# Weight sums made by adding transfers, with their products half a chunk pair later, in the output projection of a hybrid decoder layer

## Chip, cores and metric

The kernel runs on one core of one Trainium2 chip. The metric is device microseconds (us) of one execution of the whole program, lower is better.

## What is computed

One decoder layer over 256 positions of width 4096: a normalized input is projected to 13,328 columns, four head groups (retention, block attention, a state-space branch, a linear recurrence) mix them, and the four gated results, together 4096 wide, go through one output projection. The residual is added and a last RMSNorm follows. The change lies in the output projection alone, the last two lines here:

```python
h = rms_norm(x, norm_w)
proj = jnp.einsum('bsd,de->bse', h, w_in)
...
y = jnp.concatenate([y_ret, y_moba, y_ssm, y_lru], axis=-1)
return x + jnp.einsum('bse,ed->bsd', y, w_out)
```

## The kernel before

Everything is float32. To use the fast matmul type fp32r, each operand is split in two fp32r halves: a high part (a copy that rounds, made by ACT) and a low part (operand less high part, made by DVE). A product takes three matmuls: high by high, low by high, high by low. `split` (L159) does this for the weights, in `high_low` (L172): ACT casts at L173, DVE subtracts at L174. The activations `yhl` are split before.

Weights stream from memory in chunks of 128 partitions by 1024 float32 columns (512 KB); a chunk is two blocks, each of 128 rows of the weight matrix by 512 of its columns. `load` (L137) issues a chunk's transfer on SP's queue into one of five buffers `raw` (`RAW`, L24), `split` turns it into a pair `whi`, `wlo`, of which there are three (`SPL` + 1). The main loop at chunk n issues first the split of chunk n+2 and the load of chunk n+5, then the matmuls of chunk n.

The output projection does two blocks of 512 output columns at once (`pair`, L834; o = 0, 2, 4, 6, from `FAST`, L31). For each of 16 steps c over the contraction there are two chunks, i = 0 and 1, one for each column block. A plain step multiplies both chunks by both halves of the positions: 12 matmuls of 512 columns for each chunk, 24 a step. A *fast* step (c in `FAST[o]`, 18 in all) sees the 2 by 2 blocks of activations and of weights as a matrix product of Strassen and Winograd's form: seven block products in place of eight, so 21 matmuls. It needs four sums of weight blocks, which DVE makes in place in the two raw buffers (L186, L187, L189, L191), and their own splits `thi`, `tlo` (L188, L190, L192, L193: the casts and subtractions are again those of L173 and L174). The sums of activations are made once, in `mix_y` (L769), into tiles `ys`. Every three matmuls are one call of `three` (L786 to L792).

After the 16 steps `early` (L845) has mixed the products into the residual, by two operations a chunk from the queue `side`, and `row` (L802) finishes each block. POOL's queue brings the residual x and the last norm's weights (`extra`, L822) into tiles `xres` and `fw`. The last pair (o = 6) keeps the splits of its last chunks ("hold") and does half of their products at the end, beside the norm of the other half.

A scheduler sets the order of the instructions on each engine, from the order in which the program is written and its own idea of durations; on the chip each engine takes its instructions strictly in that order, and waits where one is not ready.

Of the kernel before, what the change touches and what calls it, by code (L numbers as in the profile page):

```python
# [32 lines left out]
LATE = 13  # L33
EPS = 1e-6
# [61 lines left out]
def tile_kernel(ctx: ExitStack, tc: tile.TileContext, t: dict):  # L96
# [19 lines left out]


    chunks = []
    for gi, (what, cols) in enumerate(GROUPS):
        w = len(cols)  # L120
        for c in range(NCH):
            src = t[f"w{gi}"][c]
            if gi == 0:
                chunks += [("x", src[:, k * w:(k + 1) * w], KC * c + k, 1, w) for k in range(KC)]
            else:
                chunks.append(("in", src, KC * c, KC, w))
    for o in FAST:
        for c in range(NCH):
            for i in range(2):
                where = "fast" + "ab"[i] if c in FAST[o] else "hold" if o == NO - 2 and LATE <= c + i / 2 < LATE + 1.5 else "out"  # L130
                chunks.append((where, t["wo"][o + i, c], KC * c, KC, 512))
    raws, xraws, parts = {}, {}, {}

    def b4():
        return br.tile([P, 4, S], F32, name="b4", bufs=4)
# [23 lines left out]
    def split(n):  # L159
        if n >= len(chunks):  # L160
            return
        where, _, kt, nk, w = chunks[n]
        if where == "x":
            split_x(xraws.pop(n))
        raw = raws.pop(n)
        if where == "hold":
            hi, lo = pair_of(mixed[0], "t", 4, 1024)
        else:
            hi, lo = pair_of(wp, "w", SPL + 1, WW)
        parts[n] = hi, lo  # L170

        def high_low(h, l, raw, a, b):  # L172
            A.copy(h[:, a:b], raw[:, a:b])  # L173
            V.tensor_tensor(l[:, a:b], raw[:, a:b], h[:, a:b].bitcast(F32), ALU.subtract)  # L174

        cuts = FIRST if n == 0 else CUTS if n == 1 else ((512, 1024),) if where == "fastb" else ((0, nk * w),)
        for a, b in cuts:
            high_low(hi, lo, raw, a, b)
        if where == "fasta":
            raws["a"] = raw  # L180
        elif where == "fastb":

            ra, rb = raws.pop("a"), raw
            (ha, la), (hb, lb) = (pair_of(mixed[0], "t", 4, 1024) for _ in range(2))
            c1, c2 = slice(0, 512), slice(512, 1024)
            V.tensor_tensor(ra[:, c1], rb[:, c1], ra[:, c1], ALU.subtract)  # L186
            V.tensor_tensor(rb[:, c1], rb[:, c2], rb[:, c1], ALU.subtract)  # L187
            high_low(ha, la, ra, 0, 512)  # L188
            V.tensor_tensor(rb[:, c2], rb[:, c2], ra[:, c1], ALU.subtract)  # L189
            high_low(hb, lb, rb, 0, 512)  # L190
            V.tensor_tensor(ra[:, c2], ra[:, c2], rb[:, c2], ALU.subtract)  # L191
            high_low(hb, lb, rb, 512, 1024)  # L192
            high_low(ha, la, ra, 512, 1024)  # L193
            parts[n, "t"] = (ha, la), (hb, lb)

    def pair_of(pool, tag, bufs, size):
        return [pool.tile([P, size], F32R, name=tag + x, bufs=bufs) for x in ("hi", "lo")]
# [571 lines left out]
    def mix_y(c):  # L769
        ya, yb = yhl[KC * c], yhl[KC * c + 1]  # L770
        q = mixed[0].tile([P, 512], F32, name="ma")
        for i, y in enumerate((ya, yb)):
            V.tensor_tensor(q[:, i * 256:(i + 1) * 256], y[:, 0:256].bitcast(F32), y[:, 256:512].bitcast(F32), ALU.add)
        a11, a21, a12, a22 = (q[:, i * P:(i + 1) * P] for i in range(4))
        s = mixed[0].tile([P, 512], F32, name="mb")
        s1, s2, s3, s4 = (s[:, i * P:(i + 1) * P] for i in range(4))
        V.tensor_tensor(s1, a21, a22, ALU.add)
        V.tensor_tensor(s2, s1, a11, ALU.subtract)
        V.tensor_tensor(s3, a11, a21, ALU.subtract)
        V.tensor_tensor(s4, a12, s2, ALU.subtract)  # L780
# [13 lines left out]
    def tile_y(kt, e):  # L794
        return yhl[kt][:, e * P:(e + 1) * P], yhl[kt][:, 256 + e * P:256 + (e + 1) * P]
# [6 lines left out]
    def row(o, k, ps, xres, fw, at, a=0, b=512):  # L802

        V.tensor_tensor(xres[:, a:b], xres[:, a:b], ps[:, a:b], ALU.add)
        A.activation(ps[:, a:b], xres[:, a:b], AF.Square, accum_out=fss[:, k, at:at + 1])
        V.tensor_tensor(rs[k][:, o * 512 + a:o * 512 + b], xres[:, a:b], fw[:, a:b], ALU.mult)

    def store(k):

# [24 lines left out]
    def pair(o, n, q, r, spare):  # L834
# [5 lines left out]
        held = {}  # L840

        def add(out, a, b):
            side.append(lambda: V.tensor_tensor(out, a, b, ALU.add))  # L843

        def early():  # L845

            u = mixed[0].tile([P, 512], F32, name="ma")
            w = mixed[0].tile([P, 512], F32, name="mb")
            side.append(lambda: A.copy(u, p1))
            add(x11, x11, u)  # L850
            add(u, u, p6)
            add(w, u, p7)
            add(x12, x12, u)
            add(x12, x12, p5)
            add(x21, x21, w)
            add(x22, x22, w)
            add(x22, x22, p5)
            if end:
                add(x22, x22, q[3])

        for c in range(NCH):
            if o == 0 and 1 <= c <= len(MIX):
                mix_y(MIX[c - 1])
            for i in range(2):
                split(n + SPL)
                load(n + RAW)
                for _ in range(2):
                    if side:
                        side.popleft()()
                p = parts.pop(n)  # L870
                tt = parts.pop((n, "t"), None)
                n += 1
                if c in fast:
                    first, last = c == fast[0], c == fast[-1]
                    hl = ysum[c]
                    mix = lambda j: (hl[:, j * P:(j + 1) * P], hl[:, 512 + j * P:512 + (j + 1) * P])
                    if i == 0:
                        three(p1, tile_y(KC * c, 0), p, 0, first, last)
                        three(q[0], tile_y(KC * c + 1, 0), p, 512, False, False)
                    else:  # L880
                        three(q[1], mix(3), p, 512, False, False)
                        three(p5, mix(0), tt[0], 0, first, last)
                        three(p7, mix(2), tt[1], 0, first, last)
                        three(p6, mix(1), tt[1], 512, first, last)
                        three(q[2], tile_y(KC * c + 1, 1), tt[0], 512, False, False)
                else:
                    mms(q[i], 0, c, p, c == 0, c == NCH - 1)
                    if end and c >= LATE:
                        held[c, i] = p
# [15 lines left out]
        row(o + 1, 0, q[1], x12, fw2, NO, 256, 512)  # L905
        done()
        for c in range(LATE, NCH):
            mms(q[2], 1, c, held[c, 0], False, c == NCH - 1)
        row(o, 1, q[2], x21, fw1, o)
        for j, a in enumerate((0, 256)):  # L910
            for c in range(LATE, NCH):
                mms(spare[j], 1, c, held[c, 1], c == LATE, c == NCH - 1, a, a + 256)
# [6 lines left out]
    MIX = (7, 9, 12, 2, 4)  # L919
# [53 lines left out]
```

## Time and profile before

| what | before |
| --- | --- |
| median of 3 runs | 1558.94 us (1558.78 to 1559.57) |
| profiled execution, its own time | 1558.47 us |
| its span, first to last instruction | 1556.7 us |
| PE (matmul) busy | 1541.6 us, 99% of the span |
| DVE busy | 954.6 us, 61% |
| ACT busy | 779.3 us, 50% |
| DMA, mean over the span | 200 GB/s |

The span is read stage by stage: the output projection fills its last 340 us or so. Busy shares say which engine is full; the order of an engine's instructions, and what each waits for, say whether another engine can keep it full.

### The profile page before, as it was taken

The numbers are of one execution on the slowest core, as the hardware profiler recorded it, in microseconds if no ns is written. First come the engines' busy times: TensorE is split into PE (matmuls) and PEld (weight loads), VectorE is DVE, ScalarE is ACT, GpSimd is POOL, SyncE is SP. The second block draws the span as 40 slices with busy tenths as digits, with TensorE's granted clock in tenths as the row PEclk, the third lists the DMA queues.
The fourth block names the chain that finished last, engine by engine and source line by source line (L and its number), as shares of the span: only waits on it lengthen the run. The fifth ranks groups of instructions, "written<-read, shape, count | busy, mean of one in ns | idle before, by whom it ended". The sixth has DMA issues, their size and how long they took to land.

```text
span 1556.7 us, 19182 instructions
## 1 busy us (share of the span) xinstructions
PE 1541.6 (99%) x7202; PEld 1286.7 (83%) x7202; DVE 954.6 (61%) x1233; ACT 779.3 (50%) x1019; POOL 28.7 (2%) x56
## 2 busy tenths in 40 slices
PE   9999999999999999999999999999999999999996
PEld 8988888888888788888888888888888888888885
DVE  5564444485565644545556757444447888887878
ACT  5644444454455434444448845444446555554553
POOL 0000000000000100000000000000000000000000
PEclk9999999999999999999999999999999999999999
DMA  8965555555555655545555455555555656576764
GB/s 310 333 223 179 183 178 184 178 190 189 199 187 187 207 184 189 176 170 176 185 197 182 170 196 176 196 188 189 189 195 190 220 206 238 190 234 213 235 219 168
DMA packets 89134, 311.20 MB, mean 200 GB/s; under 512 B 10304, under 2 KB 11984, under 8 KB 89040
## 3 DMA queue, kind: packets, MB, share of 16 engines
q1 hardware_dynamic: 83808, 296.70, 54.7%
q0 software_dynamic: 3360, 10.51, 2.3%
q10 hardware_dynamic: 1872, 2.76, 0.5%
q8 instruction: 56, 0.92, 0.2%
q14 instruction: 38, 0.31, 0.1%
HBM read 305.71 MB, written 4.22 MB: 199 GB/s over the span
## 4 chain that ended last, share of the span: by engine, by line
PE 97%; DVE 1%; issue 1%; DMA 0%; ACT 0%; POOL 0%; ACTq 0%; POOLq 0%; DVEq 0%
PE pm L712 24%; PE pm L710 24%; PE pm L711 24%; PE pm L792 4%; PE pm L790 4%; PE pm L791 4%; PE pb L791 3%; PE pb L792 3%; PE pb L790 3%; PE pb L287 1%; PE pb L711 0%; PE pb L712 0%; PE pb L710 0%; DMA b<-in_xt 0%; DVE xres L843 0%
## 5 line engine op out<-in xcount | busy, mean ns | idle before, releaser
L174 DVE TENSOR_TENSOR wlo<-raw,whi 128x1024 fp32r<-128x1024 f32 (+3 forms) x545 | 650.7, 1198 | 540.3 <-ACT whi L173 518.1
L173 ACT CAST whi<-raw 128x1024 fp32r<-128x1024 f32 (+3 forms) x545 | 558.6, 1029 | 642.1 <-PE pm L711 494.8
L710 PE MATMUL pm<-whi,xT 128*128 128x512 f32 (+1 forms) x1664 | 645.7, 388 | 1.1 <-ACT whi L173 1.1
L712 PE MATMUL pm<-wlo,xT 128*128 128x512 f32 (+1 forms) x1664 | 642.4, 386 | 0.9 <-DVE wlo L174 0.9
L711 PE MATMUL pm<-whi,xT 128*128 128x512 f32 (+1 forms) x1664 | 641.7, 386 | 0.0
L712 PEld LDWEIGHTS pm<-wlo,xT 128*128 128x128 f32 x1664 | 312.5, 188 | 64.5 <-DVE wlo L174 1.7
L710 PEld LDWEIGHTS pm<-whi,xT 128*128 128x128 f32 x1664 | 312.9, 188 | 63.6 <-ACT whi L173 1.6
L711 PEld LDWEIGHTS pm<-whi,xT 128*128 128x128 f32 x1664 | 312.8, 188 | 62.0
L791 PE MATMUL pm<-whi,xT 128*128 128x512 f32 (+1 forms) x218 | 84.1, 386 | 0.0
L790 PE MATMUL pm<-whi,xT 128*128 128x512 f32 (+1 forms) x218 | 84.0, 385 | 0.0
L792 PE MATMUL pm<-wlo,xT 128*128 128x512 f32 (+1 forms) x218 | 84.0, 385 | 0.0
L791 PE MATMUL pb<-whi,xT 128*128 128x512 f32 x178 | 69.2, 389 | 0.0
L792 PE MATMUL pb<-wlo,xT 128*128 128x512 f32 x178 | 69.2, 389 | 0.0
L790 PE MATMUL pb<-whi,xT 128*128 128x512 f32 x178 | 69.2, 389 | 0.0
L173 ACT CAST thi<-raw 128x512 fp32r<-128x512 f32 (+1 forms) x75 | 45.8, 636 | 33.1 <-DVE raw L186 19.9
L174 DVE TENSOR_TENSOR tlo<-raw,thi 128x512 fp32r<-128x512 f32 (+1 forms) x75 | 52.0, 708 | 0.2
L790 PEld LDWEIGHTS pm<-whi,xT 128*128 128x128 f32 x218 | 41.0, 188 | 8.2
L791 PEld LDWEIGHTS pm<-whi,xT 128*128 128x128 f32 x218 | 41.0, 188 | 8.2
L792 PEld LDWEIGHTS pm<-wlo,xT 128*128 128x128 f32 x218 | 41.0, 188 | 8.1
L791 PEld LDWEIGHTS pb<-whi,xT 128*128 128x128 f32 x178 | 33.4, 188 | 7.0
L792 PEld LDWEIGHTS pb<-wlo,xT 128*128 128x128 f32 x178 | 33.4, 188 | 7.0
L790 PEld LDWEIGHTS pb<-whi,xT 128*128 128x128 f32 x178 | 33.4, 188 | 7.0
(252 smaller groups left out, 957.4 us busy)
## 6 DMA issues: line engine op xcount, KB each, us to landing
raw<-in_w SPq DMA_DIRECT2D x384, 512.0 KB, 3.5
raw<-in_wo SPq DMA_DIRECT2D x128, 512.0 KB, 5.0
raw<-in_w SPq DMA_DIRECT2D x31, 520.0 KB, 4.5
b<-in_x SPq DMA_DIRECT2D x8, 512.0 KB, 5.5
xres<-in_x POOLq DMA_DIRECT2D x16, 256.0 KB, 5.4
b<-in_xt SPq DMA_DIRECT2D x15, 257.0 KB, 4.5
fw<-in_fnw POOLq DMA_DIRECT2D x8, 256.0 KB, 5.5
out<-rs ACTq DMA_DIRECT2D x8, 256.0 KB, 2.9
```

The lines of the kernel that those rows point to most:

```text
L173: A.copy(h[:, a:b], raw[:, a:b])
L174: V.tensor_tensor(l[:, a:b], raw[:, a:b], h[:, a:b].bitcast(F32), ALU.subtract)
L287: T.transpose(ps[:, e * S + k * P:e * S + (k + 1) * P], tk[k][:, (2 * u + e) * P:(2 * u + e + 1) * P], ident)
L710: T.matmul(ps[:, :w], xh, hi[:, o:o + w], start=first, stop=False)
L711: T.matmul(ps[:, :w], xl, hi[:, o:o + w], start=False, stop=False)
L712: T.matmul(ps[:, :w], xh, lo[:, o:o + w], start=False, stop=last)
L790: T.matmul(ps, x[0], hi, start=first, stop=False)
L791: T.matmul(ps, x[1], hi, start=False, stop=False)
L792: T.matmul(ps, x[0], lo, start=False, stop=last)
```

## The change

The change does five things. (1) The lists `FAST` become 6, 8, 10, 12 for the first pair and 2, 4, 6, 8, 10, 12 for the others: 22 fast steps. (2) Two of the four weight sums of a fast step are no longer made by DVE: right behind the split of the first chunk, `split` issues two transfers on POOL's queue with `accum_op=ALU.add`, which read one block of 512 columns (256 KB) of the second chunk again from memory and add it to the first 512 columns of each raw buffer. The signs of the activation sums and of `early` are adapted. (3) The other two sums and the four splits move to `sums_of`, called at the second chunk; the four products that use them run after the plain matmuls of the following chunk, step c+1, i = 0. (4) `RAW` is 7 in place of 5, since a fast step's raw buffers are held longer; there are three pairs of `t` tiles in place of four. (5) For room, `xres` is no tile of its own but a slice of the result `rs`, and three of the held chunks of the last pair use `t` and old `ys` tiles.

```diff
-SPL, RAW, WARM = 2, 5, 28
+SPL, RAW, WARM = 2, 7, 28
...
-FAST = {0: (7, 9, 12), 2: (2, 4, 7, 9, 12), 4: (2, 4, 7, 9, 12), 6: (2, 4, 7, 9, 12)}
+FAST = {0: (6, 8, 10, 12), 2: (2, 4, 6, 8, 10, 12), 4: (2, 4, 6, 8, 10, 12), 6: (2, 4, 6, 8, 10, 12)}
...
         if where == "fasta":
-            raws["a"] = raw
-        elif where == "fastb":
-
-            ra, rb = raws.pop("a"), raw
-            (ha, la), (hb, lb) = (pair_of(mixed[0], "t", 4, 1024) for _ in range(2))
-            c1, c2 = slice(0, 512), slice(512, 1024)
-            V.tensor_tensor(ra[:, c1], rb[:, c1], ra[:, c1], ALU.subtract)
-            V.tensor_tensor(rb[:, c1], rb[:, c2], rb[:, c1], ALU.subtract)
-            high_low(ha, la, ra, 0, 512)
-            V.tensor_tensor(rb[:, c2], rb[:, c2], ra[:, c1], ALU.subtract)
-            high_low(hb, lb, rb, 0, 512)
-            V.tensor_tensor(ra[:, c2], ra[:, c2], rb[:, c2], ALU.subtract)
-            high_low(hb, lb, rb, 512, 1024)
-            high_low(ha, la, ra, 512, 1024)
-            parts[n, "t"] = (ha, la), (hb, lb)
+
+            src = chunks[n + 1][1]
+            held[n + 1] = raw, raws[n + 1]
+            for i, c in enumerate((slice(0, 512), slice(512, 1024))):
+                nc.gpsimd.dma_start(out=held[n + 1][i][:, 0:512], in_=src[:, c], accum_op=ALU.add)
+
+    def sums_of(n):
+
+        ra, rb = held.pop(n)
+        (ha, la), (hb, lb) = (pair_of(mixed[0], "t", 3, 1024) for _ in range(2))
+        c1, c2 = slice(0, 512), slice(512, 1024)
+        high_low(ha, la, ra, 0, 512)
+        V.tensor_tensor(rb[:, c2], rb[:, c2], ra[:, c1], ALU.add)
+        high_low(hb, lb, rb, 512, 1024)
+        V.tensor_tensor(ra[:, c2], ra[:, c2], rb[:, c2], ALU.add)
+        high_low(ha, la, ra, 512, 1024)
+        high_low(hb, lb, rb, 0, 512)
+        parts[n, "t"] = (ha, la), (hb, lb)
...
-            xt = fp.tile([P, 512], F32, name="xres", bufs=4)
+            xt = rs[k][:, o * 512:(o + 1) * 512]
...
             for i in range(2):
+                if c in fast and i == 1:
+                    sums_of(n)
                 split(n + SPL)
                 load(n + RAW)
...
                     else:
                         three(q[1], mix(3), p, 512, False, False)
-                        three(p5, mix(0), tt[0], 0, first, last)
-                        three(p7, mix(2), tt[1], 0, first, last)
-                        three(p6, mix(1), tt[1], 512, first, last)
-                        three(q[2], tile_y(KC * c + 1, 1), tt[0], 512, False, False)
...
-                if c == fast[-1] and i == 1:
-                    early()
+                if i == 0 and c - 1 in fast:
+
+                    first, last = c - 1 == fast[0], c - 1 == fast[-1]
+                    hl, tt = ysum[c - 1], parts.pop((n - 2, "t"))
+                    three(p5, mix(0), tt[0], 0, first, last)
+                    three(p6, mix(1), tt[1], 512, first, last)
+                    three(q[2], tile_y(KC * (c - 1) + 1, 1), tt[0], 512, False, False)
+                    three(p7, mix(2), tt[1], 0, first, last)
+                    if last:
+                        early()
```

How the scheduler places this is shown at three places, all in the pair o = 2. First DVE, before, at the fast step c = 7: `raw_10336` and `raw_10357` are its two chunks, `wlo_10442` and `wlo_10454` belong to the two chunks of step 8, `wlo_10475` to the first chunk of the next fast step, 9. In brackets stand the semaphores that a row waits for: DMAHW are loads on SP's queue, DMASW transfers on POOL's.

```order
L186 TENSOR_TENSOR raw_10336<-raw_10357,raw_10336 128x512 [waits DMAHW0_49,DVE_49]
L187 TENSOR_TENSOR raw_10357<-raw_10357 128x512 [waits DVE_49]
L174 TENSOR_TENSOR wlo_10408<-raw_10357,whi_10407 128x512 [waits PE_49,Activation_49]
L174 TENSOR_TENSOR tlo_10412<-raw_10336,thi_10411 128x512 [waits Activation_49]
L189 TENSOR_TENSOR raw_10357<-raw_10357,raw_10336 128x512 [waits DVE_49]
L174 TENSOR_TENSOR tlo_10414<-raw_10357,thi_10413 128x512 [waits Activation_49]
L191 TENSOR_TENSOR raw_10336<-raw_10336,raw_10357 128x512 [waits DVE_49]
L174 TENSOR_TENSOR wlo_10442<-raw_10375,whi_10441 128x1024 [waits DMAHW1_49,PE_49,Activation_49]
L174 TENSOR_TENSOR tlo_10414<-raw_10357,thi_10413 128x512 [waits Activation_49]
L174 TENSOR_TENSOR tlo_10412<-raw_10336,thi_10411 128x512 [waits Activation_49]
L174 TENSOR_TENSOR wlo_10454<-raw_10393,whi_10453 128x1024 [waits DMAHW2_49,PE_49,Activation_49]
L174 TENSOR_TENSOR wlo_10475<-raw_10427,whi_10474 128x1024 [waits DMAHW3_49,PE_49,Activation_49]
```

DVE makes all four sums itself, and none of these rows waits for a transfer of POOL's. The same stretch of DVE in the changed kernel, from the fast step c = 6 (`raw_10271`, `raw_10282`) to the fast step 8 (`raw_10356`, `raw_10367`); `wlo_10412` and `wlo_10438` are the chunks of step 7.

```order
L199 TENSOR_TENSOR wlo_10362<-raw_10271,whi_10361 128x1024 [waits DMAHW5_49,PE_49,Activation_49]
L199 TENSOR_TENSOR wlo_10394<-raw_10282,whi_10393 128x512 [waits DMAHW6_49,PE_49,Activation_49]
L190 TENSOR_TENSOR raw_10282<-raw_10282,raw_10271 128x512 [waits DMASW2_49,DVE_49]
L199 TENSOR_TENSOR tlo_10424<-raw_10271,thi_10423 128x512 [waits Activation_49]
L192 TENSOR_TENSOR raw_10271<-raw_10271,raw_10282 128x512 [waits DVE_49]
L199 TENSOR_TENSOR tlo_10426<-raw_10282,thi_10425 128x512 [waits PE_49,Activation_49]
L199 TENSOR_TENSOR tlo_10426<-raw_10282,thi_10425 128x512 [waits DMASW1_49]
L199 TENSOR_TENSOR wlo_10412<-raw_10312,whi_10411 128x1024 [waits DMAHW7_49,PE_49,Activation_49]
L199 TENSOR_TENSOR tlo_10424<-raw_10271,thi_10423 128x512 [waits Activation_49]
L199 TENSOR_TENSOR wlo_10438<-raw_10330,whi_10437 128x1024 [waits DMAHW0_49,PE_49,Activation_49]
L199 TENSOR_TENSOR wlo_10447<-raw_10356,whi_10446 128x1024 [waits DMAHW1_49,PE_49,Activation_49]
L199 TENSOR_TENSOR wlo_10479<-raw_10367,whi_10478 128x512 [waits DMAHW2_49,PE_49,Activation_49]
```

Two additions are gone, and the first that is left, L190, waits for the adding transfer (DMASW2). It stands before the split of both chunks of step 7.

ACT in the same stretch of the changed kernel (casts of the same chunks):

```order
L198 CAST whi_10361<-raw_10271 128x1024 [waits DMAHW5_49,PE_49,Activation_49]
L198 CAST whi_10393<-raw_10282 128x512 [waits DMAHW6_49,DVE_49,PE_49]
L198 CAST thi_10423<-raw_10271 128x512 [waits DMASW2_49]
L198 CAST thi_10425<-raw_10282 128x512 [waits DMASW1_49,DVE_49,PE_49]
L198 CAST thi_10425<-raw_10282 128x512 [waits DVE_49]
L198 CAST whi_10411<-raw_10312 128x1024 [waits DMAHW7_49,PE_49,Activation_49]
L198 CAST thi_10423<-raw_10271 128x512 [waits DVE_49]
L198 CAST whi_10437<-raw_10330 128x1024 [waits DMAHW0_49,PE_49,Activation_49]
```

ACT too takes the cast that waits for DMASW2 before the cast of step 7's first chunk, `whi_10411`.

POOL's queue of the changed kernel at the same place: the transfer into `raw_10282`, then the one into `raw_10271`, then those of steps 8 and 10.

```order
L182 DMA raw_10282<-in_wo 128x512 [waits DMAHW6_49,DMASW3_49,DMASW1_49]
L182 DMA raw_10271<-in_wo 128x512 [waits DMAHW5_49,DMASW7_49,DVE_49]
L182 DMA raw_10367<-in_wo 128x512 [waits DMAHW2_49,DMASW0_49]
L182 DMA raw_10356<-in_wo 128x512 [waits DMASW6_49,DMAHW1_49,DMASW4_49,DVE_49]
L182 DMA raw_10452<-in_wo 128x512 [waits DMAHW6_49,DMASW5_49,DMASW2_49]
```

The transfer into a step's second chunk waits for loads and older transfers alone; the one into its first chunk waits for DVE besides, that is for the subtraction that ends this chunk's own split (`wlo_10362`, `wlo_10447`).

## Rows read from the trace of the kernel before

**Rows 1.** The page: share of the span by engine, and of the chain that ended last
```profile
PE 1541.6 (99%) x7202; PEld 1286.7 (83%) x7202; DVE 954.6 (61%) x1233; ACT 779.3 (50%) x1019; POOL 28.7 (2%) x56
...
PE 97%; DVE 1%; issue 1%; DMA 0%; ACT 0%; POOL 0%; ACTq 0%; POOLq 0%; DVEq 0%
```
**Rows 2.** Windows of the output projection: busy us by engine, clock, DMA share, GB/s
```profile
1215.00:1544.00 329.00, 329.00 (x1468) 273.02 (x1468) 277.74 (x374) 171.54 (x236) 13.41 (x25) 1.00 0.61 211
...
1230.00:1310.00 80.00, 80.00 (x354) 66.25 (x353) 66.55 (x87) 42.22 (x57) 3.20 (x6) 1.00 0.60 207
1310.00:1400.00 90.00, 90.00 (x398) 74.51 (x397) 75.67 (x98) 47.80 (x67) 3.21 (x6) 1.00 0.63 220
```
**Rows 3.** Timeline of PE inside a pair: start, duration, instruction
```profile
1328.16 0.39 PE L791 MATMUL pb<-whi,xT 128*128 128x512 f32 x1
1328.39 0.39 PE L792 MATMUL pb<-wlo,xT 128*128 128x512 f32 x1
1328.61 0.39 PE L790 MATMUL pb<-whi,xT 128*128 128x512 f32 x1
```
**Rows 4.** Timeline of DVE through one fast step
```profile
1326.85 0.69 DVE L186 TENSOR_TENSOR raw<-raw 128x512 f32<-128x512 f32 x1
1327.57 0.69 DVE L187 TENSOR_TENSOR raw<-raw 128x512 f32<-128x512 f32 x1
...
1329.38 0.68 DVE L189 TENSOR_TENSOR raw<-raw 128x512 f32<-128x512 f32 x1
1329.99 0.68 DVE L174 TENSOR_TENSOR tlo<-raw,thi 128x512 fp32r<-128x512 f32 x1
1330.59 0.68 DVE L191 TENSOR_TENSOR raw<-raw 128x512 f32<-128x512 f32 x1
1331.19 1.22 DVE L174 TENSOR_TENSOR wlo<-raw,whi 128x1024 fp32r<-128x1024 f32 x1
...
1333.53 2.35 DVE L174 TENSOR_TENSOR wlo<-raw,whi 128x1024 fp32r<-128x1024 f32 x2
```
**Rows 5.** Lines of DVE in the output projection: busy, mean ns, idle before, its releaser
```profile
L174 DVE TENSOR_TENSOR wlo<-raw,whi 128x1024 fp32r<-128x1024 f32 x104 | 125.3, 1220 | 47.2 <-ACT whi L173 47.2
```
**Rows 6.** Timeline of ACT: casts of 1024 and of twice 512 columns
```profile
1329.99 1.06 ACT L173 CAST whi<-raw 128x1024 fp32r<-128x1024 f32 x1 [1.07 <-PE pb L791]
1330.95 1.14 ACT L173 CAST thi<-raw 128x512 fp32r<-128x512 f32 x2
```
**Rows 7.** Transfers on POOL's queue, by tile: xres, fw (256 KB each), last t (128 KB)
```profile
L828 POOL DMA_DIRECT2D xres<-in_x x16: 538/538/547, 1215.2 to 1464.5; - x16
...
DMA to landing us min/median/max: 3.6/5.4/8.7
...
DMA to landing us min/median/max: 4.8/5.5/7.8
...
DMA to landing us min/median/max: 3.0/3.3/3.9
```
**Rows 8.** Loads of the output projection's chunks on SP's queue, by line
```profile
L144 SPq DMA_DIRECT2D raw<-in_wo x120: 327/328/585, 1213.4 to 1526.8; - x120
...
DMA to landing us min/median/max: 3.3/5.4/8.5
```
**Rows 9.** PE's one wait for a split, at 530 us, and windows around PE's end
```profile
530.27 0.50 PE L712 MATMUL pm<-wlo,xT 128*128 128x512 f32 x1 [0.89 <-DVE wlo L174]
...
527.00:533.00 6.00, 5.11 (x23) 3.92 (x22) 6.00 (x14) 3.24 (x5) 0.00 (x0) 1.00 0.36 122
...
1544.00:1550.00 6.00, 0.58 (x5) 0.38 (x4) 5.20 (x18) 0.91 (x4) 0.54 (x1) 0.95 0.94 357
1550.00:1556.70 6.70, 0.00 (x0) 0.00 (x0) 1.92 (x5) 0.00 (x0) 0.00 (x0) 0.50 0.79 303
```

More of the change, by code (lines that the diff above doesn't have):

```diff
@@ L118, in tile_kernel @@
     chunks = []
+    done_y = {(LATE, 1): (2, 4), (LATE + 1, 0): (6, 8)}
     for gi, (what, cols) in enumerate(GROUPS):
@@ L129, in tile_kernel @@
             for i in range(2):
-                where = "fast" + "ab"[i] if c in FAST[o] else "hold" if o == NO - 2 and LATE <= c + i / 2 < LATE + 1.5 else "out"
+                where = "fast" + "ab"[i] if c in FAST[o] else "hold" if o == NO - 2 and (c, i) in done_y else "held" if o == NO - 2 and (c, i) == (LATE, 0) else "out"
                 chunks.append((where, t["wo"][o + i, c], KC * c, KC, 512))
-    raws, xraws, parts = {}, {}, {}
+    raws, xraws, parts, held = {}, {}, {}, {}
     def b4():
@@ L166, in split @@
         if where == "hold":
-            hi, lo = pair_of(mixed[0], "t", 4, 1024)
+            hi, lo = (mixed[0].tile([P, 1024], F32R, name=f"ys{c}") for c in done_y[kt // KC, n % 2])
         else:
-            hi, lo = pair_of(wp, "w", SPL + 1, WW)
+            hi, lo = pair_of(mixed[0], "t", 3, 1024) if where == "held" else pair_of(wp, "w", SPL + 1, WW)
         parts[n] = hi, lo
-        def high_low(h, l, raw, a, b):
-            A.copy(h[:, a:b], raw[:, a:b])
-            V.tensor_tensor(l[:, a:b], raw[:, a:b], h[:, a:b].bitcast(F32), ALU.subtract)
         cuts = FIRST if n == 0 else CUTS if n == 1 else ((512, 1024),) if where == "fastb" else ((0, nk * w),)
@@ L179, in split, with high_low @@
         if where == "fasta":
-            raws["a"] = raw
-        elif where == "fastb":
-            ra, rb = raws.pop("a"), raw
-            (ha, la), (hb, lb) = (pair_of(mixed[0], "t", 4, 1024) for _ in range(2))
-            c1, c2 = slice(0, 512), slice(512, 1024)
-            V.tensor_tensor(ra[:, c1], rb[:, c1], ra[:, c1], ALU.subtract)
-            V.tensor_tensor(rb[:, c1], rb[:, c2], rb[:, c1], ALU.subtract)
-            high_low(ha, la, ra, 0, 512)
-            V.tensor_tensor(rb[:, c2], rb[:, c2], ra[:, c1], ALU.subtract)
-            high_low(hb, lb, rb, 0, 512)
-            V.tensor_tensor(ra[:, c2], ra[:, c2], rb[:, c2], ALU.subtract)
-            high_low(hb, lb, rb, 512, 1024)
-            high_low(ha, la, ra, 512, 1024)
-            parts[n, "t"] = (ha, la), (hb, lb)
+            src = chunks[n + 1][1]
[13 more added lines that the diff above has]
+        parts[n, "t"] = (ha, la), (hb, lb)
+    def high_low(h, l, raw, a, b):
+        A.copy(h[:, a:b], raw[:, a:b])
+        V.tensor_tensor(l[:, a:b], raw[:, a:b], h[:, a:b].bitcast(F32), ALU.subtract)
     def pair_of(pool, tag, bufs, size):
@@ L759, in tile_kernel @@
     fp = ctx.enter_context(tc.tile_pool(name="fp", bufs=1))
-    fsm = fp.tile([P, 176], F32, name="fsm")
+    fsm = fp.tile([P, 272], F32, name="fsm")
     fss = fsm[:, 0:2 * (NO + 1)].rearrange("p (a b) -> p a b", a=2)
@@ L776, in mix_y @@
         s1, s2, s3, s4 = (s[:, i * P:(i + 1) * P] for i in range(4))
-        V.tensor_tensor(s1, a21, a22, ALU.add)
+        V.tensor_tensor(s1, a21, a22, ALU.subtract)
         V.tensor_tensor(s2, s1, a11, ALU.subtract)
         V.tensor_tensor(s3, a11, a21, ALU.subtract)
-        V.tensor_tensor(s4, a12, s2, ALU.subtract)
+        V.tensor_tensor(s4, a12, s2, ALU.add)
         hl = mixed[0].tile([P, 1024], F32R, name=f"ys{c}")
@@ L805, in row @@
         A.activation(ps[:, a:b], xres[:, a:b], AF.Square, accum_out=fss[:, k, at:at + 1])
-        V.tensor_tensor(rs[k][:, o * 512 + a:o * 512 + b], xres[:, a:b], fw[:, a:b], ALU.mult)
+        V.tensor_tensor(xres[:, a:b], xres[:, a:b], fw[:, a:b], ALU.mult)
     def store(k):
@@ L839, in pair, with add @@
         fast, end = FAST[o], o == NO - 2
-        held = {}
-        def add(out, a, b):
-            side.append(lambda: V.tensor_tensor(out, a, b, ALU.add))
+        late = {}
+        def add(out, a, b, op=ALU.add):
+            side.append(lambda: V.tensor_tensor(out, a, b, op))
         def early():
@@ L852, in early @@
             add(w, u, p7)
-            add(x12, x12, u)
+            add(x12, x12, u, ALU.subtract)
             add(x12, x12, p5)
             add(x21, x21, w)
-            add(x22, x22, w)
+            add(x22, x22, w, ALU.subtract)
             add(x22, x22, p5)
@@ L859, in early, with mix @@
                 add(x22, x22, q[3])
+        def mix(j):
+            return hl[:, j * P:(j + 1) * P], hl[:, 512 + j * P:512 + (j + 1) * P]
         for c in range(NCH):
@@ L870, in pair @@
                 p = parts.pop(n)
-                tt = parts.pop((n, "t"), None)
                 n += 1
@@ L875, in pair @@
                     hl = ysum[c]
-                    mix = lambda j: (hl[:, j * P:(j + 1) * P], hl[:, 512 + j * P:512 + (j + 1) * P])
                     if i == 0:
@@ L888, in pair @@
                     if end and c >= LATE:
-                        held[c, i] = p
+                        late[c, i] = p
                     else:
                         mms(q[2 + i], 1, c, p, c == 0, c == (LATE - 2 if end and i else NCH - 1))
-                if c == fast[-1] and i == 1:
-                    early()
+                if i == 0 and c - 1 in fast:
[7 more added lines that the diff above has]
+                        early()
         while side:
@@ L907, in pair @@
         for c in range(LATE, NCH):
-            mms(q[2], 1, c, held[c, 0], False, c == NCH - 1)
+            mms(q[2], 1, c, late[c, 0], False, c == NCH - 1)
         row(o, 1, q[2], x21, fw1, o)
@@ L911, in pair @@
             for c in range(LATE, NCH):
-                mms(spare[j], 1, c, held[c, 1], c == LATE, c == NCH - 1, a, a + 256)
+                mms(spare[j], 1, c, late[c, 1], c == LATE, c == NCH - 1, a, a + 256)
             row(o + 1, 1, spare[j], x22, fw2, NO if j else o + 1, a, a + 256)
@@ L917, in pair @@
         return n
-    MIX = (7, 9, 12, 2, 4)
+    MIX = (6, 8, 10, 12, 2, 4)
     for j, o in enumerate(FAST):
```

## The prediction

> **What bounds the kernel now.** I read the page's busy shares and its chain first, then windows of the stage that the change touches, then one engine after the other inside it. The reader should see PE at 99% of the span and 97% of the chain that ended last [rows 1]. In the output projection it is full: 329.00 of 329.00 us busy, at the full granted clock, 1.00 [rows 2]. Since a matmul's duration (0.39 us) overlaps the next one's, its price is the distance of starts: 0.226 us [rows 3], and 398 matmuls in 90 us say the same, 0.226 [rows 2]. So each matmul of 512 columns left out is worth 0.226 us, as long as the splits that feed PE come in time. They do: DVE is busy 277.74 of these 329 us, and most of its idle time before a plain split, 47.2 us, ends with ACT's cast [rows 5]. That cast waits for PE to release a pair of `whi`, `wlo` [rows 6]: the feeders are ahead of PE and are held back by it. In order of time they still have only three pairs to run ahead with, so a wait of several us on DVE or ACT goes through to PE. That is where I look for the cost of this change.
>
> All sums are made against the profiled execution, 1558.47 us, which is its span of 1556.7 us and 1.8 us around it; it stands 0.5 us under the median of the three runs, 1558.94 us.
>
> **What the change removes.** Four more fast steps, each 21 matmuls in place of 24: 4 x 3 x 0.226 = 2.7 us off PE. That is all that PE can win, 0.17%, and it is less than the 0.2%, or 3.1 us, that a measurement of this kernel can tell from no change. On DVE two additions of 512 columns go from each fast step, 0.60 us apiece by the distance of starts [rows 4], so 36 x 0.60 = 22 us over the old 18 steps. They win nothing, because DVE is not what PE waits for.
>
> **What it adds.** 44 transfers of 256 KB, 11.5 MB, with 0.54 us of POOL each [rows 7]. Over 329 us that is 35 GB/s more beside 211 GB/s, at a DMA share of 0.61 [rows 2]: no bound by itself. What counts is the wait. I follow one period of two steps, a fast one and the plain one behind it, in the order printed above.
>
> PE has in a period: 6 matmuls of the fast step's first chunk, 3 of the second, 12 of the plain step's first chunk, then 12 products with sums, then 12 of its second chunk: 45 x 0.226 = 10.2 us.
>
> DVE and ACT have a ring to go round. The adding transfer into a step's first raw buffer starts when DVE has ended that chunk's own split. It lands L later. Until then DVE stands at L190 and ACT at the cast of `thi`, and both stand before the splits of the next plain step. They have one thing to do meanwhile, the half split of the second chunk (0.6 us). From the landing on DVE does nine instructions until it ends the first split of the next fast step, which starts the next adding transfer: six of 512 columns at 0.60 us (two additions, four subtractions), two of 1024 at 1.13 us (2.35 less 1.22), and the last of 1024 with its full 1.22 us [rows 4]. That is 3.6 + 2.3 + 1.2 = 7.1 us, and with a hand-over at each end I take 7.2 us. ACT keeps ahead of this: three casts of 512 at 0.55 and one of 1024 at 1.06 [rows 6] are 2.7 us after the landing, when DVE, five instructions on at 3.0 us, wants its result.
>
> So a period cannot be shorter than L + 7.2 us, and PE stalls for L + 7.2 - 10.2 = **L - 3.0 us in each fast step**. This is no cover that runs out once: each stall delays the next split, and with it the next transfer.
>
> **How long is L?** The trace of before has no adding transfer. Nearest are POOL's own transfers of 256 KB in this very stage: 3.6 us from issue to landing at best, 5.4 in the median, 8.7 at most (`xres`), and 4.8, 5.5 and 7.8 for `fw` [rows 7]. The short end is such a transfer with little beside it, the long one belongs to bursts of six on POOL's queue. An adding transfer goes alone or as the second of two on that queue, which speaks for less than the median; but when DVE resumes it frees several raw buffers at once, so the loads of SP's queue (median 5.4 us in this stage [rows 8]) will be under way beside it, and it has to read its destination as well, which speaks for more. I take the median, **L = 5.4 us**. A bound below is 3.6 us. Above, I allow the second reading the price of a further 256 KB in the same queue: doubling from 128 KB (3.3 us, under lighter traffic) to 256 KB (5.4 us) costs 2.1, so 7.5 us.
>
> The sum: 22 x (5.4 - 3.0) = 52.8 us of new stalls, less 2.7 us of matmuls: +50.1 us, **1608.6 us**, 3.2% slower. With L = 3.6 it is 22 x 0.6 - 2.7 = +10.5, 1569.0 us; with L = 7.5, 22 x 4.5 - 2.7 = +96.3, 1654.8 us. The first fast step of a pair has no step before it in the ring, but its first split waits for PE at the same distance; I count all 22 alike. A cast that comes late on ACT would add some tenths to each.
>
> Here the page "DMA: Bandwidth & Descriptors" of the Trainium skill, section "Anatomy of one DMA — SWDGE (gpsimd) path", speaks for the change: it puts such a transfer at 2.0 us and the bytes by 436 GB/s, so my estimate from that page is 2.6 us for 256 KB, and then no step would stall. None of the 24 transfers of that size in the trace came in under 3.6 us [rows 7], which is why I keep the rows' value.
>
> **The rest, at nothing.** `RAW` of 7: loads of a fast step's buffers are issued only when the sums are done, but a chunk so loaded is wanted seven chunks, some 15 us, later, and a load lands in 5.4 us [rows 8]; the cover is PE's work on three steps. The first five loads at the start keep their places, so the in-projection stays. `xres` in `rs`: POOL's transfers of x wait for nothing any more; `fw` still waits for the rows of the pair before, and the first adding transfer stands behind it on POOL, but DVE ends those rows before it reaches that step's split, so nothing is later. The end: `early` starts one chunk later and its ten operations fit the five chunks left at two a chunk, so the rows behind start as before; I allow 0.7 us, one DVE operation, either way.
>
> **The rivals.** (a) *The transfer is hidden.* If L is at most 3.0 us the ring is no longer than PE's 10.2 us, no step stalls, and what is left is the 2.7 us: 1555.8 us, not slower. For it: the products stand 12 matmuls, 2.7 us, later than before. Against: 3.0 us is the best of POOL's 128 KB transfers, not of 256 KB ones [rows 7]. The Trainium skill's page "DMA: Bandwidth & Descriptors", in the section named above, would have it so. Chance 0.09. It counts as "no change" mostly, as faster where some tenths at the end come on top. (b) *The adding transfer costs far more than a copy*, at or above the longest row: L = 8.7 gives 22 x 5.7 - 2.7 = +122.7, 1681 us. For: it shares the engines with bunched loads. Against: two in flight on POOL's queue, not six. Chance 0.06. (c) *The stalls cost PE its clock.* After PE's last matmul the granted clock is at 0.50 of full speed, 1.2 GHz, in the stretch from 1550 us on [rows 9]. If each stall halved it for the 24 matmuls behind, 24 x 0.226 = 5.4 us more a step: 1608.6 + 22 x 5.4 = 1727 us. Against: the wait at 530 us left it at 1.00 [rows 9]. Chance 0.04.
>
> **How the numbers follow.** My forecast, stalls of 0.6 to 4.5 us in each fast step, has 0.81, rival (a) 0.09, (b) 0.06, (c) 0.04. The predicted time is the forecast's, 1608.6 us. The range is the forecast's, from L = 3.6 to 7.5 with 2 us and 7 us more at its ends for the tenths named above: 1567 to 1662 us; it leaves out the rivals, 0.19. Slower by over 0.2% (above 1562 us) are the forecast, (b) and (c): 0.81 + 0.10 = 0.91, less 0.02 for an L just above 3.0: 0.89. Within 0.2%: that 0.02 and two thirds of (a), 0.08 in sum. Faster: the rest of (a), 0.03.
>
> **What would show it.** In the changed profile: L182 with 44 transfers, and their time to landing, which is L; DVE's idle time before L190 ended by that transfer, about L - 0.6 in each of 22 steps, some 105 us; ACT's before `thi` likewise; PE idle some 2.4 us in each fast step before the first matmuls of the plain step, ended by ACT's or DVE's split of `whi`, `wlo`, not by `thi`; a granted clock still near 1.00. Wrong would be: PE without gaps at L over 3.6 us (then the ring is mis-read), gaps before the products with sums instead, or L outside 3.6 to 7.5.

## The result, and the profile after

The changed kernel takes 1645.66 us in the median of 5 runs (1639.64 to 1649.97) against 1559.45 us (5 runs): a ratio of 1.0549, 95% interval 1.0536 to 1.0563. That is 86 us slower; the forecast was 50 us slower, and its range, 1567 to 1662 us, holds the time. The profiled execution took 1645.66 us, with a span of 1643.9 us. Two lines of its page, the busy shares and the chain that ended last, answer to [rows 1]:

```profile
PE 1573.6 (96%) x7190; PEld 1298.0 (79%) x7190; DVE 943.3 (57%) x1228; ACT 784.3 (48%) x1036; POOL 67.2 (4%) x100
...
PE 80%; DMA 8%; DVE 6%; issue 4%; ACT 1%; POOL 0%; POOLq 0%; ACTq 0%; DVEq 0%
```

PE's share of the chain fell from 97% to 80%. DMA, 0% before, has 8%, and nearly all of that is transfers of weights into `raw`. Windows of the output projection (stretch, length, busy us, with the number of instructions, of PE, of PEld, which loads PE's weights, of DVE, ACT and POOL, granted clock, DMA share, GB/s) show where PE's time went:

```profile
1230.00:1310.00 80.00, 68.73 (x276) 53.88 (x275) 51.66 (x74) 33.25 (x46) 10.13 (x13) 0.94 0.69 217
1310.00:1400.00 90.00, 74.84 (x292) 57.42 (x291) 52.63 (x69) 39.09 (x59) 10.75 (x13) 0.92 0.63 182
```

In the second one PE starts 292 matmuls where it started 398 [rows 2], and the granted clock is 0.92, not 1.00. The page's groups of lines name the waits (busy us, mean ns; idle us just before, and what ended them):

```profile
L198 ACT CAST thi<-raw 128x512 fp32r<-128x512 f32 x89 | 51.1, 621 | 135.1 <-DMA raw<-in_wo 133.8
L795 PE MATMUL pm<-whi,xT 128*128 128x512 f32 (+1 forms) x206 | 83.9, 407 | 20.9 <-ACT whi L198 20.8
L795 PE MATMUL pb<-whi,xT 128*128 128x512 f32 x166 | 70.9, 427 | 23.9 <-ACT whi L198 23.9
...
L190 DVE TENSOR_TENSOR raw<-raw 128x512 f32<-128x512 f32 x22 | 15.2, 692 | 115.9 <-DMA raw<-in_wo 115.9
```

DVE stands 115.9 us before L190, ACT 133.8 us before the cast of `thi`, both until an adding transfer lands, 22 times each. PE then waits for the cast of `whi`: a plain step's weights, not the sums. POOL's timeline (start, us, instruction), and the view of L182 with the time of all 44 transfers from issue to landing:

```profile
1332.78 0.87 POOL L182 DMA_DIRECT2D raw<-in_wo  x1 [11.87 <-DVE wlo L199]
1336.66 0.86 POOL L182 DMA_DIRECT2D raw<-in_wo  x1 [3.02 <-DMA raw<-in_wo]
1346.17 0.87 POOL L182 DMA_DIRECT2D raw<-in_wo  x1 [8.65 <-DVE wlo L199]
1351.18 0.87 POOL L182 DMA_DIRECT2D raw<-in_wo  x1 [4.14 <-DMA raw<-in_wo]
1360.71 0.86 POOL L182 DMA_DIRECT2D raw<-in_wo  x1 [8.66 <-DVE wlo L199]
```

```profile
DMA to landing us min/median/max: 3.9/5.3/10.1
```

The issues at 1332.78, 1346.17 and 1360.71 are those into a fast step's first buffer. DVE's timeline over that stretch shows one whole round:

```profile
1333.19 0.69 DVE L199 TENSOR_TENSOR wlo<-raw,whi 128x512 fp32r<-128x512 f32 x1 [0.88 <-ACT whi L198]
1338.77 0.69 DVE L190 TENSOR_TENSOR raw<-raw 128x512 f32<-128x512 f32 x1 [4.89 <-DMA raw<-in_wo]
1339.38 0.69 DVE L199 TENSOR_TENSOR tlo<-raw,thi 128x512 fp32r<-128x512 f32 x1
1339.98 0.68 DVE L192 TENSOR_TENSOR raw<-raw 128x512 f32<-128x512 f32 x1
1340.59 0.68 DVE L199 TENSOR_TENSOR tlo<-raw,thi 128x512 fp32r<-128x512 f32 x1
1341.19 1.22 DVE L199 TENSOR_TENSOR wlo<-raw,whi 128x1024 fp32r<-128x1024 f32 x1
1342.32 1.28 DVE L199 TENSOR_TENSOR tlo<-raw,thi 128x512 fp32r<-128x512 f32 x2
1343.53 2.95 DVE L199 TENSOR_TENSOR wlo<-raw,whi 128x1024 fp32r<-128x1024 f32 x3
1353.31 0.69 DVE L190 TENSOR_TENSOR raw<-raw 128x512 f32<-128x512 f32 x1 [6.83 <-DMA raw<-in_wo]
```

Issue at 1332.78, L190 6.0 us later, and 7.4 us from there to the issue at 1346.17: 13.4 us, where PE has 10.2 us of matmuls. The next round is 7.1 + 7.4 = 14.5 us. On PE's timeline the lack shows like this:

```profile
1355.89 0.50 PE L795 MATMUL pb<-whi,xT 128*128 128x512 f32 x1 [3.62 <-ACT whi L198]
...
1357.59 0.80 PE L797 MATMUL pb<-wlo,xT 128*128 128x512 f32 x1 [0.50 <-DVE wlo L199]
1358.18 0.63 PE L795 MATMUL pb<-whi,xT 128*128 128x512 f32 x1
1358.61 0.63 PE L796 MATMUL pb<-whi,xT 128*128 128x512 f32 x1
```

After the wait the matmuls stand 0.43 us apart, not 0.226. Windows of that stretch and an earlier one:

```profile
1326.40:1333.20 6.80, 6.12 (x14) 4.39 (x15) 5.92 (x9) 4.39 (x7) 0.42 (x1) 0.50 0.52 165
1357.10:1360.50 3.40, 2.91 (x7) 2.33 (x8) 3.31 (x4) 1.16 (x2) 0.00 (x0) 0.51 0.78 241
```

Twelve such stretches, 54.6 us in all, run at half the full clock, 1.2 GHz, each beginning within 2 us of a wait's end. From the projection's first matmul to its last it is now 423.6 us, before it was 337.1: 333.4 us at full pace, 65.5 us of waits, 24.0 us that matmuls lost to the half clock, and 0.7 us of rest (summed over the distances of starts).

### The profile page after: what moved, and what is told of

It reads as the page before. It is cut to its first block, busy times and chain, and to the rows that moved or that the text cites. A ratio compares the mean times of both kernels' runs of the same rounds, so it can differ in the third digit from the quotient of the medians.

```text
span 1643.9 us, 19312 instructions
## 1 busy us (share of the span) xinstructions
PE 1573.6 (96%) x7190; PEld 1298.0 (79%) x7190; DVE 943.3 (57%) x1228; ACT 784.3 (48%) x1036; POOL 67.2 (4%) x100
## 4 chain that ended last, share of the span: by engine, by line
PE 80%; DMA 8%; DVE 6%; issue 4%; ACT 1%; POOL 0%; POOLq 0%; ACTq 0%; DVEq 0%
PE pm L717 22%; PE pm L715 22%; PE pm L716 22%; DMA raw<-in_wo 7%; DVE wlo L199 2%; PE pb L797 1%; PE pm L797 1%; PE pb L795 1%; PE pb L796 1%; PE pb L292 1%; PE pm L796 1%; PE pm L795 1%; DVE tlo L199 1%; DVE raw L192 1%; DVE raw L190 1%
## 5 line engine op out<-in xcount | busy, mean ns | idle before, releaser
L198 ACT CAST thi<-raw 128x512 fp32r<-128x512 f32 x89 | 51.1, 621 | 135.1 <-DMA raw<-in_wo 133.8
L190 DVE TENSOR_TENSOR raw<-raw 128x512 f32<-128x512 f32 x22 | 15.2, 692 | 115.9 <-DMA raw<-in_wo 115.9
L795 PEld LDWEIGHTS pb<-whi,xT 128*128 128x128 f32 x166 | 34.0, 205 | 34.4 <-ACT whi L198 28.1
L199 DVE TENSOR_TENSOR tlo<-raw,thi 128x512 fp32r<-128x512 f32 x89 | 58.8, 689 | 0.0
L182 POOL DMA_DIRECT2D raw<-in_wo x44 | 38.6, 908 | 310.1 <-DVE wlo L199 175.1
## 6 DMA issues: line engine op xcount, KB each, us to landing
rs<-in_x POOLq DMA_DIRECT2D x16, 256.0 KB, 10.1
```

What stands on the lines that cost most here:

```text
L182: nc.gpsimd.dma_start(out=held[n + 1][i][:, 0:512], in_=src[:, c], accum_op=ALU.add)
L190: V.tensor_tensor(rb[:, c2], rb[:, c2], ra[:, c1], ALU.add)
L795: T.matmul(ps, x[0], hi, start=first, stop=False)
```

## The experiments

My theory before the first run was the forecast's ring: adding transfer, DVE's wait, nine instructions, next adding transfer. The rivals were a cost by the number or the traffic of the transfers, the change's later products, and PE's clock.

**All four sums on DVE, no transfers.** Everything else stays as changed.

```
-            for i, c in enumerate((slice(0, 512), slice(512, 1024))):
-                nc.gpsimd.dma_start(out=held[n + 1][i][:, 0:512], in_=src[:, c], accum_op=ALU.add)
...
+        V.tensor_tensor(ra[:, c1], ra[:, c1], rb[:, c1], ALU.add)
+        V.tensor_tensor(rb[:, c1], rb[:, c1], rb[:, c2], ALU.add)
         high_low(ha, la, ra, 0, 512)
```

> The changed kernel without the 44 adding transfers: DVE makes all four sums, all else (22 fast steps, products half a step later, seven raw buffers, three t pairs) as in the change. Ring theory (DVE and ACT stand still, in order, until the transfer into the first buffer lands, and that sets the period of two steps): no stall is left, so 1558.5 - 2.7 = 1555.8 us, 1554 to 1558. Rival (the later products, the fewer t tiles or the longer held raw buffers cost the time): it stays above 1600 us.

Measured: 1559.11 us, ratio 0.9998 (0.9989 to 1.0007). All 86 us hang on the 44 transfers; the later products, the seven raw buffers and the residual in `rs` cost nothing that shows. But the 2.7 us of saved matmuls do not show either: after a fast step PE's matmuls come some tenths late here and there, 2.7 us in all against 1.0 us before.

**One transfer.** Only the one into the second raw buffer stays; the other three sums are DVE's.

```
-            for i, c in enumerate((slice(0, 512), slice(512, 1024))):
-                nc.gpsimd.dma_start(out=held[n + 1][i][:, 0:512], in_=src[:, c], accum_op=ALU.add)
+            nc.gpsimd.dma_start(out=held[n + 1][1][:, 0:512], in_=src[:, 512:1024], accum_op=ALU.add)
```

> Only the transfer into the second chunk's buffer is kept, the one that waits for no split; DVE makes the other three sums from it (one addition more than in the change, one fewer than before). Ring theory: this transfer is issued as soon as its loads have landed, long before its sum is wanted, so no stall: 1555.8 us, 1554 to 1560. Rival (any adding transfer of this kind stalls DVE by its 5 us or so): 22 x 2 us or more of stalls, above 1600 us.

Measured: 1561.29 us, ratio 1.0017 (1.0008 to 1.0026), slightly over what I gave it. Twenty-two adding transfers whose buffer needs no split first, and whose sum is wanted last, cost 2 us, not half of 86.

**All transfers, into a tile that nobody reads.** DVE makes the sums.

```
-                nc.gpsimd.dma_start(out=held[n + 1][i][:, 0:512], in_=src[:, c], accum_op=ALU.add)
+                nc.gpsimd.dma_start(out=spares[0][:, c], in_=src[:, c], accum_op=ALU.add)
```

> All 44 adding transfers run, same source, bytes and place in the program, but they add into a tile that nobody reads; DVE makes the four sums. Ring theory: traffic without a wait costs nothing, as the first run of this study, 1554 to 1560 us. Rival (contention: 11.5 MB more and POOL's queue make the loads late): a good part of the 86 us remains, 1580 us or more, and the casts of plain chunks wait for loads.

Measured: 1566.82 us, ratio 1.0053 (1.0039 to 1.0066). The traffic alone is not the 86 us. Most of the 8 us over the run without transfers is one wait; PE's row, then two of DVE's:

```profile
1389.20 0.79 PE L801 MATMUL pm<-wlo,xT 128*128 128x512 f32 x1 [5.89 <-DVE wlo L201]
```

```profile
1375.59 1.22 DVE L201 TENSOR_TENSOR wlo<-raw,whi 128x1024 fp32r<-128x1024 f32 x1 [0.17 <-ACT whi L200]
1385.52 1.29 DVE L815 TENSOR_TENSOR rs<-rs,fw 128x512 f32<-128x512 f32 x2 [8.71 <-DMA fw<-in_fnw]
```

DVE stood at a row's end until `fw` had landed; POOL had issued `fw` only at 1379.92, behind these transfers, which wait for each other in their one tile.

**Twelve more matmuls per fast step,** of a zero tile, 60 us of work for PE, so that its work in a round, 12.9 us, comes near the round's length and it stands less.

```
+                        for _ in range(12):
+                            T.matmul(q[1], zero, p[0][:, 512:1024], start=False, stop=False)
```

> The changed kernel with 12 matmuls more in each fast step (264 in all, 264 x 0.227 = 59.9 us of PE work), with a zero operand, which add nothing, just ahead of PE's stall. Ring theory with the ring alone: PE has 12.9 us of work in a period of some 13.8, so the time does not move by more than 5 us: 1640 to 1650. Ring theory plus clock (the stalls of the changed kernel let PE's clock fall to 0.50 in places, and that costs the 13 us that 22 x (6.2 + 7.5 - 10.2) = 77 leaves open): the clock stays near 1.00 and the time falls to 1630 to 1640. Rival (PE's work is on the path all the time): 1645.7 + 60 = 1705.

Measured: 1680.4 us, ratio 1.0776, a miss. 25 of the 60 us were absorbed, but PE still stood. The order of POOL's transfers had come out differently: the one into the second buffer, which waits for a late load, stood ahead of the one into the first, so the round became longer too. So it settles nothing on the clock.

**Copies in place of adding transfers.** The two sums that they would make are left out.

```
-                nc.gpsimd.dma_start(out=held[n + 1][i][:, 0:512], in_=src[:, c], accum_op=ALU.add)
+                nc.gpsimd.dma_start(out=held[n + 1][i][:, 0:512], in_=src[:, c])
```

> The 44 transfers copy instead of adding, into the same places with the same waits; the two sums they would make are left out, so this run computes something else. Ring theory: a round of the ring is the landing time L plus the 7.5 us of DVE's nine instructions, against 10.2 us of PE, and only L can change. If the adding itself costs (adding transfers in the ring landed in about 6.2 us, the residual's copies before in a median of 5.4), the time falls by 22 x 0.8 = 18 us of stall and some of the 24 us at half clock, to 1615 to 1630; if the adding is free, the time stays within 5 us of the change's 1645. Rival, that an adding transfer is dear in itself (reads its destination and holds DMA engines longer): L falls to about 3.6 us and the time to 1575 to 1590.

Measured: 1620.27 us, ratio 1.039 (1.0372 to 1.0407), inside the ring's numbers. The time of these copies from issue to landing:

```profile
DMA to landing us min/median/max: 2.8/4.1/9.4
```

For the transfers into the first buffer, from issue to DVE's L190 it was 5.0 us in the mean of 22 (3.4 to 6.9), with the adding transfers 6.2 us (5.2 to 7.5). Adding costs 1.2 us more than copying, 22 x 1.2 = 26 us, and the time fell by 25. The transfers into the second buffer differ by as much, 4.7 us against 3.5. Of the 1.2 us, 0.33 are POOL's own issue, 0.87 us against 0.54. Some 70% of the loss stays with nothing added: what costs is the wait, whatever lands.

**Sums and products half a pair later.**

```
-                if c in fast and i == 1:
-                    sums_of(n)
                 split(n + SPL)
...
+                if c - 1 in fast and i == 0:
+                    sums_of(n - 1)
```

(and the products at `i == 1`; the call now stands ahead of the split two steps on.)

> The four sums' splits and the seven products stand half a chunk pair later still; the transfers and DVE's nine instructions between landing and next issue stay in one ring. Ring theory: a buffer's round is as long as before, so PE stalls as much per fast step: 1630 to 1655. Rival, that the products merely stand too early (PE waits for splits which half a pair more would have covered): the 65 us of waits go, 1560 to 1580.

Measured: 1633.82 us, ratio 1.048 (1.0465 to 1.0496): the ring's number. The scheduler, though, had put L190 straight behind the fast step's half split again, as DVE's timeline shows, with its waits before L190 in all:

```profile
1332.18 0.69 DVE L199 TENSOR_TENSOR wlo<-raw,whi 128x512 fp32r<-128x512 f32 x1
1338.82 0.69 DVE L190 TENSOR_TENSOR raw<-raw 128x512 f32<-128x512 f32 x1 [5.95 <-DMA raw<-in_wo]
```

```profile
DVE raw L190 <- DMA raw<-in_wo: 115.4, 22, 7.2
```

So this moved the products and not the wait. Its 18 rounds inside the pairs are 13.5 us in the mean, 13.9 in the change, which is 7 of the 12 us between the two; the rest is open.

**Three apart, four apart.** `FAST` with every third or every fourth chunk, and the tables that follow from it; shown is the second.

```
-FAST = {0: (6, 8, 10, 12), 2: (2, 4, 6, 8, 10, 12), 4: (2, 4, 6, 8, 10, 12), 6: (2, 4, 6, 8, 10, 12)}
+FAST = {0: (6, 10), 2: (2, 6, 10), 4: (2, 6, 10), 6: (2, 6, 10)}
```

> Seven-product chunks stand three apart, 15 of them instead of 22, 30 adding transfers. Ring theory: a round is L + 7.5 + two more splits of 1.14 = 16.0 us at L = 6.2, and PE has 69 matmuls x 0.226 = 15.6 us: a stall of at most 0.4 us a round, 6 us in all, no stretch at half clock to speak of, and three fast steps fewer than before, 9 matmuls or 2.0 us more: 1560 to 1572. Rival, that the transfers cost by their number (traffic on the DMA engines or their waits, whatever the distance): 30/44 of the change's 86 us, so about 1620.

> Seven-product chunks stand four apart, 11 of them, 22 adding transfers. Ring theory: a round of 18.2 us against 93 matmuls x 0.226 = 21.0 us of PE: no stall; seven fast steps fewer than before are 21 matmuls or 4.8 us more: 1561 to 1567. Rival by the number of transfers: half of 86 us, about 1602.

Measured: 1611.25 us, ratio 1.033 (1.0314 to 1.0345), and 1592.93 us, ratio 1.0219 (1.0203 to 1.0234). The ring fails here, and the rival's numbers, 1620 and 1602, are near. Waits per fast step are 41.6/15 = 2.8 and 28.1/11 = 2.6 us, almost the 65.5/22 = 3.0 of the change, though a round four apart, with the 4.1 us of the rows below (4.4 in the mean of 11), 4.1 + 7.5 + 4 x 1.14 = 16.2 us, has 5 us to spare against PE's 93 x 0.227 = 21.1. What holds PE up is seen in ACT's timeline of the run four apart, and in PE's:

```profile
1332.62 1.05 ACT L198 CAST whi<-raw 128x1024 fp32r<-128x1024 f32 x1 [1.67 <-PE pb L796]
1335.35 0.62 ACT L198 CAST whi<-raw 128x512 fp32r<-128x512 f32 x1 [1.67 <-PE pb L796]
1339.31 0.62 ACT L198 CAST thi<-raw 128x512 fp32r<-128x512 f32 x1 [3.34 <-DMA raw<-in_wo]
```

```profile
1339.91 0.39 PE L797 MATMUL pb<-wlo,ys 128*128 128x512 f32 x1
1340.93 0.50 PE L795 MATMUL pb<-whi,xT 128*128 128x512 f32 x1 [0.63 <-ACT whi L198]
...
1342.46 0.50 PE L797 MATMUL pb<-wlo,xT 128*128 128x512 f32 x1 [0.80 <-DVE wlo L199]
```

The fast step's first cast starts at 1332.62, when PE frees a pair. From there PE has 12 + 12 + 6 + 3 = 33 matmuls before it wants the next plain chunk, which is as far as three pairs let the feeders run ahead: 33 x 0.227 = 7.5 us, and it runs out at 1340.1. The feeders need 2.6 us to the transfer's issue (1335.23), 4.1 us until it lands (1339.31) and about 3 us until the plain step's `wlo` is done: 9.7 us. The stall of some 2 us comes once per fast step at any distance, because three pairs hold no more lead, however idle DVE was before. So the second theory, of **lead**: what counts is how much work for PE stands split ahead of the place where DVE and ACT wait. It explains the counts as well as the rival does, so the next runs keep every transfer and move only the wait.

**The sums held behind the plain step's splits.** On top of the later products, the sums' instructions on ACT and DVE are tied, in issue order, behind both splits of the next plain step.

```
-                    sums_of(n - 1)
+                    with tc.issue_after(behind[0]), tc.issue_after(behind[1]):
+                        sums_of(n - 1)
```

> All 22 steps and 44 adding transfers as in the change, but the sums' casts and DVE instructions are held, in issue order, behind both splits of the next plain step, and their products stand half a chunk pair later. Theory of lead (the three pairs of split weights are what PE lives on while DVE and ACT stand; where the wait stands in their order decides, not the number or the distance of the transfers): PE has 57 matmuls or 12.9 us between the split that starts a transfer and the products, against 2.6 us to issue, L, and 4.6 us for the sums: a stall only where L is over 5.7 us; 1556 to 1572. Rival, cost by the number of transfers whatever waits for them: near the change's 1645, at least 1620. Rival, the ring of the forecast with the sums in it (L + 3.6 + 1.2 + 0.5 us, 11.5 at L = 6.2, against 10.2): 22 x 1.3 us, 1583 to 1600.

> The same hold of the sums behind the next plain step's splits, with 11 seven-product chunks four apart and 22 transfers. Theory of lead: the 28 us of waits of the run four apart go, what is left is 21 matmuls more than before, 4.8 us: 1561 to 1567. Rival, cost by the number of transfers: 1593 as with the sums in their old place.

Measured with all 22 steps and 44 adding transfers: **1560.18 us, ratio 1.0006 (0.9997 to 1.0015)**. Four apart: 1566.03 us, 1.0039 (1.0026 to 1.0053), its 4.8 us of extra matmuls and 2 more. Both as the lead theory said; the rival by number is out. DVE's timeline of the first of these:

```profile
1344.58 1.22 DVE L199 TENSOR_TENSOR wlo<-raw,whi 128x1024 fp32r<-128x1024 f32 x1
1348.34 2.36 DVE L199 TENSOR_TENSOR wlo<-raw,whi 128x1024 fp32r<-128x1024 f32 x2 [2.54 <-ACT whi L198]
1350.62 0.69 DVE L199 TENSOR_TENSOR tlo<-raw,thi 128x512 fp32r<-128x512 f32 x1
1351.22 0.69 DVE L190 TENSOR_TENSOR raw<-raw 128x512 f32<-128x512 f32 x1
```

Two plain splits and the next fast step's first split now stand ahead of `tlo` and L190, and L190 waits for nothing, though the landing is no quicker. Its adding transfers, and a window of the same stretch:

```profile
DMA to landing us min/median/max: 4.3/5.2/10.4
```

```profile
1310.00:1400.00 90.00, 90.00 (x397) 74.07 (x396) 70.77 (x92) 49.18 (x70) 12.49 (x15) 1.00 0.86 244
```

PE is full again, at a clock of 1.00, with a DMA share of 0.86.

**The same order with the sums on DVE** and no transfers, by the two pieces of code shown.

> The order of the run with the sums behind the plain step's splits, but all four sums made by DVE and no adding transfer. If the small gaps that eat the 2.7 us of saved matmuls come from splits that are just in time after a fast step (theory), holding the sums back removes the gaps of some tenths: span 1554 to 1555.5, 0.1% under before. If the output projection simply gives them back elsewhere (rival), it stays where the run with the sums on DVE in the old order was, a span of 1556 to 1557.5, and the 44 transfers of the run before this cost nothing of their own.

Measured: 1567.07 us, ratio 1.005 (1.0036 to 1.0063), a miss of both. The trace names no wait of PE; its matmuls come mostly 0.05 to 0.11 us late at some sixty places, with DVE busy 78.7 us of 90. In this order, then, the adding transfers are worth 7 us to DVE. Why these small delays arise is open. No run was faster than the kernel before.

## Why the prediction was right, and where it was off

**Direction, place and mechanism were right.** DVE's nine instructions between landing and next issue, ACT and DVE standing before the plain step's splits, PE's waits ended by `whi` and `wlo`: all as written. DVE's wait came out at 115.9 us for "some 105", PE's at 3.0 us a step for 2.4.

**The sum's terms were too small.** In the 18 rounds inside the pairs the time from one first-buffer issue to the next is 13.9 us in the mean, 3.7 us over PE's 10.2, and 18 x 3.7 = 67 us. The forecast had 5.4 + 7.2 = 12.6 us. L was the larger miss, 6.4 us to L190 in these rounds (6.2 over all 22) for 5.4: the copy run shows that a copy in this place takes 5.0 us, so the rows of copies [rows 7] were a fair price for a copy, and what lacked was 1.2 us for the adding, which the text named and put only in the upper bound. DVE's part was 7.5 us for 7.2. "0.54 us of POOL each" was a copy's price too: an adding transfer took 0.87 us. By the Trainium skill's page "DMA: Bandwidth & Descriptors", section "Anatomy of one DMA — SWDGE (gpsimd) path", my estimate was 2.6 us; no adding transfer landed under 3.9, and no copy in its place under 2.8: the measured times decide.

**"I count all 22 alike" failed.** 87.2 us of span, plus the 2.7 saved, less the rounds' 67, leaves 23 us for the four pairs' first steps and ends, 5.7 us each for 2.4. This is the loss of 90 us that PE's waits and its half clock add up to as well, counted by rounds. "Nothing is later" on POOL's queue failed too: the 16 transfers of x no longer wait for the rows of the pair before, and all go out at the start,

```profile
L833 POOL DMA_DIRECT2D rs<-in_x x16: 536/537/908, 1215.8 to 1234.5; - x16
```

and the adding transfer issued among them at 1230.46 took the longest of all, 10.1 us.

**That the range held is in part luck.** With the measured 6.2 us the forecast's own sum gives 1558.47 + 22 x 3.2 - 2.7 = 1626 us, 20 us under the measured time. Those 20 us are mostly DVE's 0.3 us a round and the pairs' first steps and ends. The range took them in because its upper end allowed an L of 7.5 us in every step, and only the slowest of the 22 came to that.

**The clock.** "A granted clock still near 1.00" was wrong: rival (c) happened in part, and PE lost 24 us to the half clock. They do not seem to come on top of the ring, as (c) had it: the issues at 1319.67 and 1332.78 are 13.1 us apart with 6.4 us of half clock between them, the next 13.4 us with 0.5. Twelve of the 18 rounds hold over 3 us at half clock and last 14.2 us in the mean, the other six 13.4; but 0.6 of these 0.7 us lie between the issue and L190 (6.6 us against 6.0), where DVE waits for the transfer. Where the round is set by the transfer, a slow PE would only stand less. I read this from the rounds and no run shows it: the one meant to test it did not.

**The rule itself was too narrow.** "If L is at most 3.0 us the ring is no longer than PE's 10.2 us, no step stalls" takes the round for the only limit. Three and four apart show another: the lead of three pairs must cover the one wait. The forecast's first paragraph has this ("a wait of several us on DVE or ACT goes through to PE"), but the sum left it out; two apart, the rounds of 13.9 us against 10.2 account for most of the loss without it, so the sum could stand. What the lead alone would have cost there was not measured.

**Rivals.** (a) and (b) did not happen. That 2.7 us could be won on PE was not borne out: the shortest distance from first to last matmul of any run is 336.7 us, with the sums on DVE in the change's order, 0.4 us under the kernel before.

## What to carry to other kernels

Before a wait is added to an in-order engine that also feeds the bottleneck, ask what stands behind it there: the same transfers cost 86 us in front of the next splits and 1 us behind them. Test a stall against two limits, the period of the loop that it closes and the lead that the buffers hold across it; more distance between the steps cures only the first. When a scheduler orders the engines, look where the waiting instruction really came to stand, since moving its call in the source may move nothing.

## What the runs showed of the hardware that I had not expected

The granted clock fell to 0.50 in the middle of the projection, in twelve stretches that begin close to waits of PE of mostly 2 to 5 us; with waits cut to some tenths it stayed at 1.00. The wait's length alone does not tell: after two waits of 2.4 and 2.1 us, at 1382.74 and 1395.91, it did not fall. An adding transfer of 256 KB took 1.2 us more than a copy in the same place, into either buffer. And in the run with the sums held back the DMA share from 1310 to 1400 us was 0.86, where it had been 0.63 before the change [rows 2], with no loss to PE.
